# Grouped-query units moved beside the state-space scans, neighbourhood heads beside the Fourier mixer, weighted sums in float32

## The chip, the cores and the metric

The kernel runs on one core of a Trainium2 chip. Its engines each work through their own instructions in order: TensorE (PE, with its weight loads as PEld), VectorE (DVE), ScalarE (ACT), GpSimd (POOL), and SyncE (SP), which here issues DMAs. The metric is the device time of one execution in microseconds (us); lower is better.

## What is computed

Two layers of a hybrid block over 1,024 latent tokens and 256 context tokens (1,280 in all, ten tiles of 128), width 1,024. Each layer mixes tokens in four groups of 256 channels which share one input and one output projection, then runs an MLP:

```python
z = modulate(rms_norm(x, g_pre_mix), sh1, sc1) @ w_in         # latent; zc likewise for the context
oa = gqa_mixer(z, ...)      # A: 4 query heads on 2 key/value heads, softmax(q k) v, 64 channels a head
ob = s5_mixer(z, ...)       # B: 16 groups of 16 channels, 64 complex states, scan in both directions, GELU + GLU
on = na_mixer(z, ...)       # C: 4 heads, each query sees 8 x 16 grid neighbours (with a bias) and the context
od = fourier_mixer(z, ...)  # D: real 2-D DFT over positions and channels, then a linear map
y = jnp.concatenate([oa, ob, on, od], axis=-1) @ w_out
x = x + g1 * rms_norm(y, g_post_mix)
x = x + g2 * rms_norm(sq_relu_mlp(modulate(...), w_mlp1, w_mlp2), g_post_mlp)
```

Attention is a softmax of scores and then a weighted sum of the values `v`. The context's own outputs are needed in layer 0 only.

## The kernel before

Everything is computed to float32 accuracy. Most matmuls reach it by splitting each operand into a rounded high part and a low part, both of type fp32r, and adding three products (high x high, high x low, low x high), as in `mm3` (L157 to L162). ScalarE rounds (`copy`, L148), VectorE or GpSimd subtracts (`sub`, L151). S5's small matmuls are plain float32.

`run()` goes through a layer in stages: norm, input projection (with the preparation of S5's tables woven in), the middle stage, output projection (which starts with S5's gate matmuls, the GLU), MLP. The middle stage is what the change touches. It has two parts:

- `attention` works through *units*. A grouped unit G(j, b) is key/value head j with 512 queries of two query heads (b = 2: the 256 context queries, layer 0 only); an N(h) is one neighbourhood head. The order is `G(0,0), N(0), G(0,1), G(0,2), N(1), G(1,0), N(2), G(1,1), G(1,2), N(3)`. A unit's preparation (`gqa_prep`, `na_prep`: splitting, transposes, row maxima of the scores) is woven into the unit ahead of it. In a unit's main part (`gqa_main`, `na_main`), for each of ten key tiles: two fp32r score matmuls per 512 columns (L657, L795), the exponential on ScalarE (L658, L799) into `e`, and `weights`, which makes a rounded `eh` (ScalarE; every third key tile of a grouped unit VectorE, L607) and `el = e - eh` (shared by GpSimd and VectorE). One and two key tiles later `pv` issues three fp32r matmuls per block of 512 columns (L624, L625, L629) into the accumulator; `va` and `vl` are the values' high and low parts, and columns of ones in `va` make the softmax denominators. `finish` sends the denominators through memory and back with three DMAs (rt, den, rden), with a reciprocal between them, and multiplies.
- `s5_scan` then takes two of the 16 S5 groups at a time, beside the Fourier mixer `fnet` and the last unit's `finish`. `front` loads tables `v`, `cs`, `sn` by DMA on ScalarE's queue, multiplies (L1268), rotates, swaps the halves of the partitions, scans, rotates back; `rear` of a group comes two fronts later and makes its output with three matmuls (L1304, L1306).

`fnet` also fills the last unit's main part. The final order on each engine is that of a list scheduler with an internal timeline, given priorities in the code; score tiles have three PSUM banks (`ps_open("A", 3)`). After the stage the output projection loads its weights (`raw`, L170) on SP and splits them into `wh` and `wl`.

Of the kernel before, what the change touches and what calls it, by code (L numbers as in the profile page):

```python
# [26 lines left out]
NEG = -1.0e30  # L27
MAGIC = 12582912.0
# [3 lines left out]
class K:  # L32
# [72 lines left out]
    def ps_open(self, which, s1=0):  # L105
# [7 lines left out]
        if which == "A":  # L113
            self.psA, self.s1 = pool, s1
        else:
            self.psM = pool
# [336 lines left out]
    CM = [(part, off + m * 128, m) for part, off in (("naq", 768), ("nak", 1024), ("s5", 512), ("fn", 1536)) for m in range(2)]  # L453
# [32 lines left out]
    def qk_prep(self, p, ps, zg, t, cosr, sinr, gqk, h0):  # L486
# [12 lines left out]
        self.copy(zg[:, t, 384:512], ps[:, 384:512])  # L499
# [33 lines left out]
    def attn_set(self, p, nq, name, others=()):  # L533


        nc = self.nc
        s = {n: p.tile([128, w], F32R, name=name + n) for n, w in (("k1", TOK), ("k2", TOK), ("q1", nq), ("q2", nq))}
        for tag, w in others:
            p.tile([128, w], F32, tag=tag, bufs=1, name=tag)
        s["va"] = p.tile([128, NT, 128], F32R, name=name + "va")  # L540
        s["vl"] = p.tile([128, NT, 64], F32R, name=name + "vl")
        nc.gpsimd.memset(s["k2"][64:128, :].bitcast(F32), 0.0)
        nc.gpsimd.memset(s["k2"][64:65, :].bitcast(F32), 1.0)
        nc.gpsimd.memset(s["va"][:, :, 64:128].bitcast(F32), 1.0)
        return s

    def gqa_prep(self, st, u):

        nc, pb, s, zg = self.nc, st["pb"], st["g"], st["zg"]
        j, b, t0, n = u["j"], u["b"], u["t0"], u["n"]  # L550
        k1, k2, va, vl = s["k1"], s["k2"], s["va"], s["vl"]
        if b == 0:
# [8 lines left out]
            src = zg[:, :, 384 + 64 * j:448 + 64 * j]  # L561
            self.copy(va[:, :, 0:64], src)
            self.sub(vl, src, va[:, :, 0:64].bitcast(F32), nc.gpsimd)
# [8 lines left out]
        q1, q2 = st["c"] if b == 2 else (s["q1"], s["q2"])  # L572
# [27 lines left out]
        u["q"] = (q1, q2)  # L600
# [42 lines left out]
    def gqa_main(self, st, u, o):  # L643
        nc, pa, s = self.nc, st["pa"], st["g"]
        q1, q2 = u["q"]
        w = u["n"] * 128
# [1200 lines left out]
```

## Time and profile before

| | us |
|---|---|
| median of three runs | 3164.7 (3159.8 to 3165.99) |
| the profiled execution | 3155.56 |
| its span, first to last instruction | 3153.8 |
| TensorE busy | 2907.9 (92% of the span) |
| VectorE / ScalarE / GpSimd busy | 1824.3 / 1197.7 / 1194.1 |
| mean granted TensorE clock | 0.963 of full speed |

The median is over whole executions, the profile is one of them. Busy times are sums over the span and say nothing on their own of which engine others wait for; the middle stage takes 376.5 us of layer 0 and 343.5 us of layer 1 up to the output projection's first matmul.

### The profile page before, as it was taken

To read this page: it belongs to the slowest core of one execution; us is meant where nothing else is said; L and a number is where in the kernel's file an instruction comes from. 1 tells how busy PE (TensorE), PEld (TensorE's weight loads), DVE (VectorE), ACT (ScalarE), POOL (GpSimd) and SP (SyncE) were. 2 spreads that over 40 slices of the span, in tenths; PEclk is the share of its full clock that TensorE was granted. 3 is DMA by queue.
4 is the path that set the end of the run, shared out by engine and by line. 5 is a ranking of instruction groups with operands and counts; after the bars stand their busy time and mean duration, and the time that the engine had idled before them with its cause. 6 is when DMAs were issued, how large, how long until landed. Compare 5 with 4: busy or idle time off the path is not lost. (4 is left out here: it accounts for less than half of the span.)

```text
span 3153.8 us, 39690 instructions
## 1 busy us (share of the span) xinstructions
PE 2907.9 (92%) x15120; PEld 2450.9 (78%) x15120; DVE 1824.3 (58%) x2368; ACT 1197.7 (38%) x1932; POOL 1194.1 (38%) x951
## 2 busy tenths in 40 slices
PE   6999888789999999999999889878689999999998
PEld 3788666577888889888988788756577788888887
DVE  3465787586676544655554784689675334433334
ACT  3443666664322222332222244556663321212212
POOL 2474466445522122512212564466645211111113
PEclk8999999889999999999999999989889999999999
DMA  7534312562444432533333444411563211111113
GB/s 270 174 126 124 75 51 54 126 199 101 161 153 132 129 96 72 167 105 105 117 103 108 149 130 125 90 55 50 132 204 100 87 41 53 44 50 54 48 47 107
DMA packets 234723, 340.11 MB, mean 108 GB/s; under 512 B 50756, under 2 KB 170916, under 8 KB 234532
## 3 DMA queue, kind: packets, MB, share of 16 engines
q1 hardware_dynamic: 223268, 320.26, 33.0%
q10 hardware_dynamic: 11264, 17.31, 1.9%
q8 instruction: 119, 1.95, 0.3%
q14 instruction: 72, 0.59, 0.1%
HBM read 283.78 MB, written 53.62 MB: 107 GB/s over the span
## 5 line engine op out<-in xcount | busy, mean ns | idle before, releaser
L148 ACT ACTIVATE wh<-raw 128x1024 fp32r<-128x1024 f32 x234 | 242.6, 1056 | 787.2 <-PE ps L162 553.3
L160 PE MATMUL ps<-mh,wh 128*128 128x320 f32 (+1 forms) x1536 | 519.5, 338 | 9.4 <-DVE y L154 6.4
L162 PE MATMUL ps<-mh,wl 128*128 128x320 f32 (+1 forms) x1536 | 517.8, 337 | 0.9 <-DVE wl L151 0.9
L161 PE MATMUL ps<-ml,wh 128*128 128x320 f32 (+1 forms) x1536 | 518.1, 337 | 0.0
L154 DVE TENSOR_TENSOR y<-ps,y 128x1024 f32<-128x1024 f32 (+1 forms) x253 | 306.4, 1219 | 261.7 <-PE ps L162 261.5
L160 PE MATMUL ps<-wh,hidh 128*128 128x512 f32 x1152 | 452.0, 393 | 2.1 <-DVE y L154 2.1
L162 PE MATMUL ps<-wh,hidl 128*128 128x512 f32 x1152 | 448.2, 390 | 2.9 <-POOL hidl L151 2.9
L161 PE MATMUL ps<-wl,hidh 128*128 128x512 f32 x1152 | 449.7, 390 | 0.0
L151 POOL TENSOR_TENSOR hidl<-r,hidh 128x640 fp32r<-128x640 f32 (+1 forms) x128 | 189.3, 1479 | 679.0 <-DVE r L154 679.0
L151 DVE TENSOR_TENSOR wl<-raw,wh 128x1024 fp32r<-128x1024 f32 x188 | 289.2, 1551 | 167.4 <-ACT wh L148 162.9
L160 PEld LDWEIGHTS ps<-mh,wh 128*128 128x128 f32 x1536 | 290.2, 189 | 35.0 <-issue 7.3
L162 PEld LDWEIGHTS ps<-mh,wl 128*128 128x128 f32 x1536 | 289.9, 189 | 21.5 <-DVE wl L151 1.5
L161 PEld LDWEIGHTS ps<-ml,wh 128*128 128x128 f32 x1536 | 290.0, 189 | 20.7
L151 POOL TENSOR_TENSOR el<-e,eh 128x640 fp32r<-128x640 f32 (+7 forms) x164 | 250.5, 1540 | 131.7 <-ACT eh L148 44.7
L151 POOL TENSOR_TENSOR wl<-raw,wh 128x1024 fp32r<-128x1024 f32 x48 | 119.3, 2485 | 470.7 <-ACT wh L148 470.5
L160 PEld LDWEIGHTS ps<-wh,hidh 128*128 128x128 f32 x1152 | 216.8, 188 | 53.0 <-issue 5.8
L162 PEld LDWEIGHTS ps<-wh,hidl 128*128 128x128 f32 x1152 | 216.6, 188 | 49.1 <-POOL hidl L151 3.8
L161 PEld LDWEIGHTS ps<-wl,hidh 128*128 128x128 f32 x1152 | 216.8, 188 | 43.2
L154 DVE TENSOR_TENSOR r<-r 128x640 f32<-128x640 f32 (+1 forms) x128 | 96.7, 756 | 241.7 <-ACT hidh L1493 241.6
L1491 ACT ACTIVATE r<-ps 128x640 f32<-128x640 f32 (+1 forms) x128 | 82.3, 644 | 366.4 <-PE ps L162 360.2
L293 DVE SCALAR_TENSOR_TENSOR acc<-raw,cst,acc 128x1024 f32<-128x1024 f32 x70 | 98.0, 1424 | 139.2 <-DMA raw<-in_w_ada_dram 139.2
L151 DVE TENSOR_TENSOR el<-e,eh 128x384 fp32r<-128x384 f32 (+4 forms) x164 | 150.4, 926 | 42.7 <-ACT eh L148 25.9
(395 smaller groups left out, 5929.6 us busy)
## 6 DMA issues: line engine op xcount, KB each, us to landing
raw<-in_w_mlp_dram SPq DMA_DIRECT2D x192, 512.0 KB
raw<-in_w_ada_dram SPq DMA_DIRECT2D x96, 512.0 KB
raw<-in_w_in_dram SPq DMA_DIRECT2D x28, 512.0 KB
x<-x SPq DMA_DIRECT2D x26, 512.0 KB
x<-h SPq DMA_DIRECT2D x18, 512.0 KB
x<-in_x_dram SPq DMA_DIRECT2D x16, 512.0 KB
raw<-in_w_out_dram SPq DMA_DIRECT2D x16, 512.0 KB
bq<-in_na_bq_dram SPq DMA_DIRECT2D x8, 800.0 KB
```

The source lines that it names most:

```text
L148: self.nc.scalar.activation(out, in_, AF.Copy, scale=scale)
L151: (eng or self.nc.vector).tensor_tensor(out=out, in0=a, in1=b, op=OP.subtract)
L154: (eng or self.nc.vector).tensor_tensor(out=out, in0=a, in1=b, op=op)
L160: self.nc.tensor.matmul(ps, ah, bh, start=start and i == 0, stop=False)
L161: self.nc.tensor.matmul(ps, ah, bl, start=False, stop=False)
L162: self.nc.tensor.matmul(ps, al, bh, start=False, stop=stop and i == n - 1)
L293: nc.vector.scalar_tensor_tensor(acc[c], x, col, acc[c], op0=OP.mult, op1=OP.add)
L1491: nc.scalar.activation(r.rearrange("p (b n) -> p b n", b=nb), ps[:, :nb, :w], AF.Relu)
```

## The change

Five things change, all in the middle stage:

- Units run as all grouped ones first, then the four heads. Keys and queries have tiles of their own for each j and b, and heads have two sets in turn (`na_set`).
- The weighted sum is one float32 matmul per block on `e` itself. `weights`, `va` and `vl` go. The ones for the denominators are a 65th column beside each head's values, in `zg` and in `vf`.
- S5 works on one group at a time (16 steps), on single PSUM banks, and all its DMAs are issued by SP. A step of it follows every second step of a grouped unit; what is left is drained ahead of the unit that prepares the first head.
- `fnet` gets a step after every third step of a head. The last head's `finish` is drained at the end of `attention`.
- Scores have two PSUM banks instead of three; other tiles of one bank alternate between two pools. The input projection makes S5's columns ahead of the heads' (`CM`).

The diff, cut to its core:

```diff
-        pool, bufs = self.psM, 2
         if tag == "s1":
             pool, bufs = self.psA, self.s1
-        elif self.s1 == 3:
+        else:
+            where = self.p1[self.p1n % len(self.p1)]
             self.p1n += 1
-            if self.p1n % 3 == 0:
-                pool, bufs = self.psA, 1
+            pool, bufs = (self.psA if where == "A" else self.psM), 2
...
-    CM = [(part, off + m * 128, m) for part, off in (("naq", 768), ("nak", 1024), ("s5", 512), ("fn", 1536)) for m in range(2)]
+    CM = [(part, off + m * 128, m) for part, off in (("s5", 512), ("naq", 768), ("nak", 1024), ("fn", 1536)) for m in range(2)]
...
+    def na_set(self, pn, i):
+        nc = self.nc
+        s = dict(zip(("k1", "k2", "q1", "q2"), (*self.keys(pn, f"n{i}"), *self.queries(pn, f"n{i}", TOK))))
+        s["vf"], s["bt"] = pn.tile([128, NT, 65], F32, name=f"nvf{i}"), pn.tile([128, 23, 64], F32, name=f"nbt{i}")
...
-    def weights(self, pa, e, n, vec, lo):
-        eh = pa.tile([128, 1024], F32R, tag="eh", bufs=3, name="eh")[:, :n]
-        if vec:
-            self.nc.vector.tensor_copy(eh, e)
-        else:
-            self.copy(eh, e)
-        el = pa.tile([128, 1024], F32R, tag="el", bufs=3, name="el")[:, :n]
-        c = int(n * lo) // 64 * 64
-        self.sub(el[:, :n - c], e[:, :n - c], eh[:, :n - c].bitcast(F32), self.nc.gpsimd)
-        if c:
-            self.sub(el[:, n - c:], e[:, n - c:], eh[:, n - c:].bitcast(F32))
-        return eh, el
-    def pv(self, queue, s, kt, parts, start, stop):
-        mm = self.nc.tensor.matmul
-        def high():
-            for po, eh, el in parts:
-                mm(po, s["va"][:, kt, :], eh, start=start, stop=False)
-                mm(po[0:64], s["vl"][:, kt, :], eh, start=False, stop=False)
-        def low():
-            for po, eh, el in parts:
-                mm(po, s["va"][:, kt, :], el, start=False, stop=stop)
-        queue += [(2, high), (3, low)]
+        yield
+    def pv(self, queue, vf, kt, parts, start, stop):
+        def whole():
+            for po, e in parts:
+                self.nc.tensor.matmul(po[0:65], vf[:, kt, :], e, start=start, stop=stop)
+        queue.append((2, whole))
...
-            eh, el = self.weights(pa, e, 2 * w, kt % 3==1, 0.4)
-            parts = [(po[:, h * 512:h * 512 + w], eh[:, h * w:(h + 1) * w], el[:, h * w:(h + 1) * w]) for h in range(2)]
-            self.pv(queue, s, kt, parts, kt == kts[0], kt == NT - 1)
+            self.pv(queue, vf, kt, [(po[:, h * 512:h * 512 + w], e[:, h * w:(h + 1) * w]) for h in range(2)],
+                          kt == kts[0], kt == NT - 1)
...
-            eh, el = self.weights(pa, e, n, False, 0.3)
-            parts = [(po[:, x:y], eh[:, x - ra * 64:y - ra * 64], el[:, x - ra * 64:y - ra * 64]) for x, y in pieces]
-            self.pv(queue, s, kt, parts, i == 0, i == 9)
+            cols = [(po[:, x:y], slice(x - ra * 64, y - ra * 64)) for x, y in pieces]
+            self.pv(queue, s["vf"], kt, [(x, e[:, c]) for x, c in cols], i == 0, i == 9)
...
-        units = [G(0, 0), N(0), G(0, 1), G(0, 2), N(1), G(1, 0), N(2), G(1, 1), G(1, 2), N(3)]
+        units = [dict(kind="g", j=j, b=b, t0=4 * b, n=4 if b < 2 else 2) for j in range(2) for b in range(3)]
+        units += [dict(kind="n", h=h, nq=nq) for h in range(NA_HEADS)]
...
-    def attention(self, pa, fp, st, o, mid, late):
+    def attention(self, l, st, o, fnet):
...
+        sp = self.open(f"s5{l}")
+        side, every = self.s5_scan(sp, l), 2
+        self.ps_open("A", 2, "AM")
...
+            if sp is not None and any(units[k]["kind"] == "n" for k in ahead):
+                for _ in side:
+                    pass
+                sp.release()
+                sp = None
+                pn = st["pn"] = self.open(f"attN{l}")
+                st["n"] = [self.na_set(pn, 0)]
+            if i == ng:
+                for p in (pc, st["pb"], st["zp"]):
+                    p.release()
+                pa = self.open(f"attO{l}")
+                st["n"].append(self.na_set(pa, 1))
+                self.ps_open("A", 2, "A")
+                self.ps_open("M")
+                side, every = fnet, 3
...
-            if i + 1 < len(units):
-                self.weave(main, self.early(itertools.chain(*ahead), 600), 3)
-            else:
-                late = late()
-                for k, _ in enumerate(main):
-                    if k % self.late[1] < self.late[0]:
-                        next(late, None)
-        return st["fin"]
+            main = self.every(main, side, every)
+            self.weave(main, self.early(itertools.chain(*(self.attn_prep(st, k) for k in ahead)), 600), 3)
...
+        for _ in st["fin"]:
+            pass
...
+    def every(main, other, n):
+        for i, x in enumerate(main):
+            if i % n == n - 1:
+                next(other, None)
+            yield x
...
+        def front(g):
+            v, cs, sn = (p.tile([128, 2, w], F32, tag=n, bufs=2, name=n) for n, w in (("v", 128), ("cs", 160), ("sn", 160)))
             for t, n in ((v, "v"), (cs, "cs"), (sn, "sn")):
-                nc.scalar.dma_start(t, dr[n][:, g0:g0 + nb])
-            pv = self.ps2(tag="pS")
+                nc.sync.dma_start(t, dr[n][:, g])
...
-            nc.scalar.dma_start(dr["y"][g0:g0 + nb].rearrange("g p c -> p g c"), y)
+            nc.sync.dma_start(dr["y"][g], y)
...
-        for g0 in range(0, 16, nb):
-            st = (g0, front(g0))
-            if g0 < 2 * nb:
-                xs.append(outs(g0))
-            if g0 == nb:
-                t0 = p.tile([128, 16, 128], F32, tag="s5t0", bufs=1, name="s5t0")
+        for g in range(16):
+            st = (g, front(g))
+            if g < 2:
...
-            fnet, self.ftags = self.early(self.fnet(l, o), 100), ("pM",)
-            def late():
-                self.ps_open("M")
-                pb.release()
-                zp.release()
-                return fnet
-            self.ps_open("A", 3)
-            with self.pool(f"attA{l}") as pa:
-                fin = self.attention(pa, up, st, o, lambda: self.s5_load(s5u, l), late)
+            self.ftags = ("pM",)
+            st["zp"] = zp
+            self.attention(l, st, o, self.early(self.fnet(l, o), 100))
             self.ps_open("A")
-            self.npS, self.ftags = 1, ("pM", "pF")
-            with self.pool(f"s5{l}") as p:
-                for i, _ in enumerate(self.along(self.s5_scan(p, l, s5u), fin)):
-                    if i % self.mix == 0:
-                        next(fnet, None)
```

What moves on the engines. The first place is TensorE in layer 0's first grouped unit, before; `gq`/`gk` are queries and keys, numbers tell tiles apart, `nk`, `nq` belong to the next head's preparation.

```order
L629 MATMUL ps<-el,gva 128x512 x2
L657 MATMUL ps<-gq_2775,gk_2773 128x512
L657 MATMUL ps<-gq_2776,gk_2774 128x512
L624 MATMUL ps<-eh,gva 128x512
L625 MATMUL ps<-eh,gvl 64x512
L624 MATMUL ps<-eh,gva 128x512
L625 MATMUL ps<-eh,gvl 64x512
L657 MATMUL ps<-gq_2775,gk_2773 128x512
L657 MATMUL ps<-gq_2776,gk_2774 128x512
L748 MATMUL ps<-nk_3291,nq_3293 128x512
L629 MATMUL ps<-el,gva 128x512 x2
```

After, TensorE in layer 0's second grouped unit (`g0q`, `g0k` its queries and keys; `zg` holds values and ones; `s5u`, `v`, `z` are S5's input, table and scanned states, `z` of three tiles used in turn).

```order
L1268 MATMUL ps<-s5u,v 128x160 x2
L1299 MATMUL ps<-s5u,s5tm 128x160
L1301 MATMUL ps<-z_3352,x_3555 128x160 x2
L1268 MATMUL ps<-s5u,v 128x160 x2
L1299 MATMUL ps<-s5u,s5tm 128x160
L641 MATMUL ps<-g0q_2778,g0k_2774 128x512
L641 MATMUL ps<-g0q_2779,g0k_2775 128x512
L641 MATMUL ps<-g0q_2778,g0k_2774 128x512
L641 MATMUL ps<-g0q_2779,g0k_2775 128x512
L611 MATMUL ps<-e,zg 65x512 x2
L520 MATMUL ps<-identr,qhh 128x128 x4
L1301 MATMUL ps<-z_3350,x_3633 128x160 x2
```

Per block one float32 row on `e`,`zg` stands where rows with `eh` and `el` stood, and S5's rows stand among them: L1268 is the first matmul of a group, L1299 and L1301 are the last ones of an earlier group. The last row is of the group whose L1268 row is eight rows above the excerpt.

The second place is TensorE in S5 before, in layer 0:

```order
L1304 MATMUL ps<-s5u,s5tm 128x160
L1306 MATMUL ps<-z_6290,x_6332 128x160 x2
L1304 MATMUL ps<-s5u,s5tm 128x160
L1306 MATMUL ps<-z_6290,x_6332 128x160 x2
L1268 MATMUL ps<-s5u,v 128x160 x4
```

There, S5's rows stand by themselves, two groups after one another (four L1268 rows at a time) and beside the Fourier mixer's.

The third place is SP at the end of layer 0's middle stage, before; `raw` are weights of the output projection, `yt` S5's outputs, `gwr` the gate's weights:

```order
L1298 DMA x_6667<-s5x_147 128x512
L170 DMA raw<-in_w_out_dram 128x1024 x4
L1339 DMA yt_6739<-s5y_149 128x1280
L1339 DMA yt_6741<-s5y_149 128x1280
L1341 DMA gwr<-in_w_s_glu_dram 128x2x256
L195 DMA rg<-mod_2_82 128x1024
L195 DMA ra<-mod_4_84 128x1024
L195 DMA rb<-mod_3_83 128x1024
L170 DMA raw<-in_w_out_dram 128x1024 x4
```

After; `rt`, `den` and `rden` are the last head's denominators on their way to memory and back:

```order
L1334 DMA yt_6218<-s5y_149 128x1280
L1334 DMA yt_6220<-s5y_149 128x1280
L665 DMA rt<-rden 128x1x10
L1336 DMA gwr<-in_w_s_glu_dram 128x2x256
L194 DMA rg<-mod_2_82 128x1024
L194 DMA ra<-mod_4_84 128x1024
L194 DMA rb<-mod_3_83 128x1024
L672 DMA den_6160<-rt 128x10
L675 DMA rden<-den_6160 64x1280
L169 DMA raw<-in_w_out_dram 128x1024 x8
```

The first four loads of weights stood ahead of S5's outputs; all eight now stand behind the last denominators.

## Rows read from the trace of the kernel before

**Rows 1.** The page, busy time of the engines over the whole span.

```profile
PE 2907.9 (92%) x15120; PEld 2450.9 (78%) x15120; DVE 1824.3 (58%) x2368; ACT 1197.7 (38%) x1932; POOL 1194.1 (38%) x951
```

**Rows 2.** Stretches: length, PE PEld DVE ACT POOL busy (count), PEclk, DMA share, GB/s.

```profile
307.50:600.00 292.50, 241.64 (x1109) 180.17 (x1107) 226.44 (x373) 188.98 (x320) 171.46 (x122) 0.92 0.26 61
600.00:684.00 84.00, 60.39 (x334) 54.01 (x334) 60.17 (x104) 44.19 (x74) 45.93 (x44) 0.78 0.71 194
307.50:684.00 376.50, 302.03 (x1443) 234.18 (x1441) 286.61 (x476) 233.16 (x393) 217.39 (x165) 0.89 0.36 91
1986.00:2250.00 264.00, 219.52 (x966) 163.17 (x965) 214.16 (x342) 165.52 (x272) 158.79 (x106) 0.92 0.26 63
2250.00:2329.50 79.50, 53.72 (x318) 47.79 (x317) 57.35 (x99) 45.32 (x72) 50.38 (x48) 0.85 0.72 197
200.00:300.00 100.00, 90.74 (x607) 83.90 (x606) 62.55 (x132) 45.35 (x104) 59.01 (x63) 0.98 0.45 132
```

**Rows 3.** TensorE groups by form, 307.5 to 684 us: count, busy us, mean ns.

```profile
L624 PE MATMUL ps<-eh,gva 128*128 128x512 f32 x80 | 32.7, 409 | 1.2 <-ACT rden L148 1.2
```

**Rows 4.** TensorE timeline in a grouped unit: start, us, engine, line, tile.

```profile
340.84 0.40 PE L624 MATMUL ps<-eh,gva 128*128 128x512 f32 x1
341.07 0.39 PE L625 MATMUL ps<-eh,gvl 128*64 128x512 f32 x1
```

**Rows 5.** TensorE timeline in S5.

```profile
663.15 0.44 PE L1304 MATMUL ps<-s5u,s5tm 128*128 128x160 f32 x2
663.42 0.71 PE L1306 MATMUL ps<-z,x 128*128 128x160 f32 x4
663.96 0.43 PE L1304 MATMUL ps<-s5u,s5tm 128*128 128x160 f32 x2
```

**Rows 6.** Groups by form, 307.5 to 684 us, all engines.

```profile
L151 POOL TENSOR_TENSOR el<-e,eh 128x640 fp32r<-128x640 f32 x40 | 69.6, 1747 | 36.5 <-ACT eh L148 17.3 <-DVE eh L607 8.0 <-PE ps L657 4.7
...
L151 DVE TENSOR_TENSOR el<-e,eh 128x384 fp32r<-128x384 f32 x40 | 48.8, 1223 | 16.3 <-ACT eh L148 9.5 <-PE ps L657 3.3 <-ACT nmt L148 2.0
L658 ACT ACTIVATE e<-ps 128x512 f32<-128x512 f32 x80 | 45.3, 596 | 33.5 <-PE ps L657 23.8 <-DVE el L151 7.6 <-issue 0.8
L148 ACT ACTIVATE eh<-e 128x1024 fp32r<-128x1024 f32 x36 | 38.3, 1063 | 3.4 <-PE ps L625 3.0
```

**Rows 7.** Waits by line and releaser, 307.5 to 684 us: total us, times, longest.

```profile
POOL el L151 <- ACT eh L148: 26.3, 15, 5.7
...
PEld ps L629 <- POOL el L151: 14.8, 10, 4.3
...
PE ps L629 <- POOL el L151: 11.6, 6, 4.1
...
PE ps L1268 <- DMA v<-s5v: 8.2, 2, 7.5
```

**Rows 8.** S5 operations by form, same view and stretch as Rows 6.

```profile
L1283 DVE TENSOR_TENSOR_SCAN gg<-r,m 128x160 f32<-128x160 f32 x32 | 18.7, 639 | 0.1
...
L154 POOL TENSOR_TENSOR g<-gg,sn 128x640 f32<-128x640 f32 x8 | 14.4, 1796 | 18.1 <-issue 11.8 <-DMA v<-s5v 5.3 <-DVE gg L1283 0.9
...
L148 ACT ACTIVATE m<-m 64x640 f32<-64x640 f32 x16 | 11.8, 735 | 4.4 <-DVE m L154 2.0 <-DVE rt L688 1.9 <-DVE gl L151 0.3
```

**Rows 9.** SP timeline, issues of DMAs in layer 0.

```profile
362.72 0.52 SPq L682 DMA_DIRECT2D rt<-rden  x1
...
367.65 0.57 SPq L692 DMA_DIRECT2D rden<-den  x1
...
674.72 1.76 SPq L170 DMA_DIRECT2D raw<-in_w_out_dram  x4
...
689.81 2.44 SPq L170 DMA_DIRECT2D raw<-in_w_out_dram  x4
```

**Rows 10.** TensorE and GpSimd timeline at the end of the stage.

```profile
678.41 1.04 POOL L181 CAST wh<-raw 128x1024 fp32r<-128x1024 f32 x1 [0.26 <-DMA raw<-in_w_out_dram]
...
687.54 0.80 PE L161 MATMUL ps<-wl,oh 128*128 128x512 f32 x1 [2.00 <-DVE wl L151]
```

More of the change, by code (lines that the diff above doesn't have):

```diff
@@ L531, in put_o, with keys, queries @@
             pos, i = pos + m * step, i + m
-    def attn_set(self, p, nq, name, others=()):
+    def keys(self, p, name):
         nc = self.nc
[L537 to L544, printed above, removed]
+        k1, k2 = (p.tile([128, TOK], F32R, name=name + n) for n in ("k1", "k2"))
+        nc.gpsimd.memset(k2[64:128, :].bitcast(F32), 0.0)
+        nc.gpsimd.memset(k2[64:65, :].bitcast(F32), 1.0)
+        return k1, k2
+    def queries(self, p, name, n):
+        return [p.tile([128, n], F32R, name=name + x) for x in ("q1", "q2")]
+    def na_set(self, pn, i):
+        nc = self.nc
+        s = dict(zip(("k1", "k2", "q1", "q2"), (*self.keys(pn, f"n{i}"), *self.queries(pn, f"n{i}", TOK))))
+        s["vf"], s["bt"] = pn.tile([128, NT, 65], F32, name=f"nvf{i}"), pn.tile([128, 23, 64], F32, name=f"nbt{i}")
+        nc.gpsimd.memset(s["q2"][64:128, :].bitcast(F32), 0.0)
+        nc.gpsimd.memset(s["vf"][:, :, 64:65], 1.0)
         return s
     def gqa_prep(self, st, u):
-        nc, pb, s, zg = self.nc, st["pb"], st["g"], st["zg"]
+        nc, pb, zg = self.nc, st["pb"], st["zg"]
         j, b, t0, n = u["j"], u["b"], u["t0"], u["n"]
-        k1, k2, va, vl = s["k1"], s["k2"], s["va"], s["vl"]
+        k1, k2 = u["k"] = st["k"][j]
         if b == 0:
@@ L571, in gqa_prep @@
         yield
-        q1, q2 = st["c"] if b == 2 else (s["q1"], s["q2"])
+        q1, q2 = u["q"] = st["q"][b]
         self.transposes(q1, lambda i: qhh[:, i // n, i % n].rearrange("p a d -> p (a d)"), 2 * n)
@@ L655, in gqa_main @@
                 hs = slice(h * w, (h + 1) * w)
-                for kk, qq in ((s["k1"], q1), (s["k2"], q2)):
-                    nc.tensor.matmul(ps, kk[:, ks], qq[:, hs], start=kk is s["k1"], stop=kk is s["k2"])
+                for kk, qq in ((k1, q1), (k2, q2)):
+                    nc.tensor.matmul(ps, kk[:, ks], qq[:, hs], start=kk is k1, stop=kk is k2)
                 nc.scalar.activation(e[:, hs], ps, AF.Exp)
@@ L730, in na_prep @@
         yield
[L731 to L734 removed]
+        mx = pn.tile([128, 8, 3], F32, tag="mx", bufs=1, name="mx")
         nc.gpsimd.memset(mx, NEG)
@@ L832, in attn_start @@
         nq = NLAT if l == self.depth - 1 else TOK
-        st = dict(l=l, pb=pb, zg=zg, g=self.attn_set(pb, 1024, "g"))
+        st = dict(l=l, pb=pb, zg=zg, k=[self.keys(pb, "g0")], q=[self.queries(pb, "g0", 1024)])
         st["ql"] = pb.tile([128, 2, 4, 128], F32R, name="ql")
         self.nc.gpsimd.memset(st["ql"][:, :, :, 64:128].bitcast(F32), 0.0)
-        G = lambda j, b: dict(kind="g", j=j, b=b, t0=4 * b, n=4 if b < 2 else 2)
-        N = lambda h: dict(kind="n", h=h, nq=nq)
-        units = [G(0, 0), N(0), G(0, 1), G(0, 2), N(1), G(1, 0), N(2), G(1, 1), G(1, 2), N(3)]
+        units = [dict(kind="g", j=j, b=b, t0=4 * b, n=4 if b < 2 else 2) for j in range(2) for b in range(3)]
+        units += [dict(kind="n", h=h, nq=nq) for h in range(NA_HEADS)]
         st["units"] = [u for u in units if u.get("b") != 2 or nq > NLAT]
@@ L844, in attn_prep @@
         return self.gqa_prep(st, u) if u["kind"] == "g" else self.na_prep(st, u)
-    def attention(self, pa, fp, st, o, mid, late):
+    def attention(self, l, st, o, fnet):
         units = st["units"]
-        nq = units[1]["nq"]
-        st["pa"], st["fp"], st["n"] = pa, fp, self.attn_set(pa, TOK, "n", (("bq", 25 * 64), ("cq1", 512), ("cq2", 512), ("bt", 23 * 64)))
-        self.nc.gpsimd.memset(st["n"]["q2"][64:128, :].bitcast(F32), 0.0)
-        st["c"] = [pa.tile([128, 512], F32R, tag=f"c{n}", bufs=1, name=f"c{n}") for n in ("q1", "q2")] if nq > NLAT else None
+        ng = sum(u["kind"] == "g" for u in units)
+        ctx = any(u.get("b") == 2 for u in units)
+        up = self.open(f"up{l}")
+        for n, w in (("oraw", TOK), ("rden", TOK), ("oraw2", 256), ("rden2", 512)):
+            up.tile([128, w], F32, tag=n, bufs=1, name=n)
+        pg = self.open(f"attG{l}")
+        st["fp"], st["pg"] = up, pg
+        pc = self.open(f"attC{l}", "right")
+        st["k"].append(self.keys(pc, "g1"))
+        st["q"].append(self.queries(pc, "g1", 1024))
+        if ctx:
+            st["q"].append(self.queries(pc, "gc", 512))
+        sp = self.open(f"s5{l}")
+        side, every = self.s5_scan(sp, l), 2
+        self.ps_open("A", 2, "AM")
         for i, u in enumerate(units):
-            if i == len(units) // 2:
-                mid()
             ahead = [] if u.get("b") == 2 else [i + 1]
@@ L1263, in front @@
+        def front(g):
+            v, cs, sn = (p.tile([128, 2, w], F32, tag=n, bufs=2, name=n) for n, w in (("v", 128), ("cs", 160), ("sn", 160)))
             for t, n in ((v, "v"), (cs, "cs"), (sn, "sn")):
[L1264 to L1265 removed]
+                nc.sync.dma_start(t, dr[n][:, g])
+            pv = self.ps1()[:, :320].rearrange("p (d c) -> p d c", d=2)
             for d in range(2):
[L1267 to L1269 removed]
@@ L1270, in front @@
-            pv = pv.rearrange("p (d c) -> p d c", d=2)[:, :, :nb * 160].rearrange("p d (g c) -> p g d c", g=nb)
-            m1, m2, m3 = (p.tile([128, nb, 2, 160], F32, tag=n + par, bufs=1, name=n) for n in ("m1", "m2", "m3"))
+                nc.tensor.matmul(pv[:, d], v[:, d, :], u[:, g, 32 * d:32 * d + 160], start=True, stop=True)
+            m1, m2, m3 = (p.tile([128, 2, 160], F32, tag=n, bufs=2, name=n) for n in ("m1", "m2", "m3"))
+            self.tt(m2, pv, sn, OP.mult)
             self.tt(m1, pv, cs, OP.mult)
-            self.tt(m2, pv, sn, OP.mult)
```

141 lines of the change are left out of this document (60 added, 81 removed).

## The prediction

> **What bounds the kernel now.** I read the page first. TensorE is busy 92% of the span and no other engine over 58% [rows 1], but that mixes stages, so I cut the span where the change acts: per layer, from the first score matmul to the moment at which the output projection's matmuls run without gaps, 307.5 to 687.5 us in layer 0 and 1986.2 to 2332.7 in layer 1 (380 and 346.5 us; by [rows 10] the first of these matmuls starts at 687.54, and the bounds in layer 1 are found in the same way). The table by stretches [rows 2] shows two things there that the input projection (200 to 300 us) does not have: a granted clock of 0.92 and 0.78 (0.92 and 0.85 in layer 1) against 0.98, and an S5 part in which TensorE is busy for 60 of 84 us.
>
> Busy time is modelled and stretches at the lower clock, so I also counted what TensorE would need at its full pace. A reduced-precision (fp32r) matmul of 512 columns starts 0.23 us after the one ahead of it [rows 4]; by the median over all neighbours it is 0.227, and 0.120 for 256 columns, 0.11 for 128. A float32 matmul leaves two records; three rows of S5 have two records of 160 columns in 0.27 us and four in 0.54 [rows 5], 0.135 each, which is two clocks a column at 2.4 GHz. With these paces the 1443 matmuls of the first window [rows 2], and the few up to 687.5, need 246 us, and layer 1's need 227. So the stage uses 65% of its time for matmuls in both layers; counted likewise, the input projection uses 85% (84.6 of 100 us). The rest is waiting: the list of waits has TensorE and its weight loads on the weights' low parts (14.8 + 11.6 us), GpSimd for the rounded weights (26.3), and S5's first matmul for a table (8.2) [rows 7]. No engine is full; they wait for one another in turn.
>
> **The change, part by part.**
>
> *Weighted sums.* Three fp32r matmuls per block of 512 columns, 3 x 0.227 = 0.681 us, become one float32 matmul of two records. By [rows 5] a 512-column record is 512 x 2 / 2.4 GHz = 0.427 us, the pair 0.854. Per layer the blocks are 80 of 512 in the grouped units [rows 3], 50 in the heads (four heads of 6,400 columns), and in layer 0 eight of 256 in each kind for the context: 138 and 130 in units of 512. TensorE pays 268 x 0.173 = 46 us: 246 becomes 270, 227 becomes 249.5. The price is bounded below by the pace of two fp32r matmuls (0.454, 61 us less than now) and above by twice the pair (1.7); 0.854 is taken, being the row's own form at another width.
>
> The Trainium skill (page "FP8 and Floating Point Precision", section "TensorE Precision Notes") has true FP32 as four passes through the array. Four passes at the fp32r pace of 0.227 would make 0.908 in place of 0.854, an estimate, and the sum 14 us dearer. No row here has a float32 matmul of 512 columns; S5's rows show two records for one matmul, not four.
>
> *What goes from the other engines.* In layer 0: 64 us of rounding copies on ScalarE (38.3 of them in one row), 90 on VectorE (48.8 in one row, the rest in narrower ones and in casts), 137 on GpSimd (69.6 in one) [rows 6]. Their load in the stage falls from 233, 287 and 217 us [rows 2] to about 170, 198 and 80. TensorE at 270 is then clearly the longest. The chain from an exponential to its weighted sum also loses a copy (1.06 us) and a subtraction (1.75 us on GpSimd).
>
> *S5 among the grouped units.* The same matmuls in pieces of one group. Its VectorE and ScalarE operations are half as wide and twice as many: a swap of 0.735 us at 640 columns becomes two of between 0.37 and 0.735; I take 0.43, so 32 x 0.125 = 4 us more per layer on ScalarE, hidden since it is not full; uncovered it would be those 4 us. VectorE's and GpSimd's halves I take as halves. One group's chain (two products, swap, difference, two scans of 0.64, product, swap, product, three sums) is about 8 us by halves of [rows 8]. In the new order a group's last matmuls stand two or three fronts behind its first, but sometimes only 5 to 8 us of matmuls, as the excerpt of the change shows: TensorE then waits in order, and score and weighted-sum matmuls behind it wait too. I allow 1 us for each of the 16 groups; it lies in the share used below.
>
> *Loads.* 64 issues of S5 tables and outputs go from ScalarE to SP, and 80 are added by halving the pieces. SP gets some 72 per layer at about 0.45 us, 32 us spread over 190. Their cover is that fronts run two groups ahead, about 12 us each. Behind a unit's denominators an S5 load can wait the 4.9 us from the one issue to the other [rows 9]; that is less than the cover, so nothing is charged. The transfers themselves move from a stretch with a DMA share of 0.71 into ones with 0.26 [rows 2]. Without cover it would be 6 units x 5 us = 30 us per layer.
>
> *Two score banks in place of three.* An exponential takes 0.60 us, a pair of score matmuls 0.45. The 1.7 us of weighted sums lies between, so it is hidden; without it, 0.15 us per bank.
>
> *Charged at nothing.* The order of the input projection's columns, tiles of their own for keys and queries, the memsets of ones, two sets for the heads: the same work or less, on engines with room, under a TensorE that is busy. Uncovered, the memsets are a few us per layer.
>
> *The end.* Before, the projection's first weights were issued at 674.72, under the last S5 groups, and the second four at 689.81 [rows 9]; the full pace came at 687.54. After, all eight stand on SP behind the last head's denominators. After the last weighted sum come copies out of the accumulator, the 4.9 us between issues, then landing (3.7 us from the issue at 674.72 to the first cast of these weights on GpSimd [rows 9, 10]), rounding and difference: about 13 us by an estimate, of which S5's gate matmuls fill 4. I charge 9 us per layer. It is between 3 (what before loses now) and 30 (denominators, S5 outputs and loads one after the other, at the lower clock after the gap).
>
> **Sum.** In layer 0 the grouped units with S5 hold 161 us of matmuls (scores 38, weighted sums 72, preparations 26, S5 22, one head's preparation 3), the heads with the Fourier mixer 109. Grouped units: many independent matmuls, other engines at 60 to 65% of it; I choose the input projection's kind of share, 86%: 187 us. Heads: bias additions, maxima and a chain of single-row copies remain, so I choose 79%, between that and the 70% which before's attention uses (203.6 us of matmuls at full pace in the 292.5 of [rows 2]): 138 us. 187 + 138 + 9 = 334, 46 less than 380. Layer 1: 151 / 0.86 + 98.5 / 0.79 + 9 = 310, 36 less. Together 82 us off the profiled execution's 3155.6, so 3073. The median of the three runs is 9 us above that execution, so 3080 to 3082 there; I say 3080. Other stages run the same work.
>
> **Rivals.**
>
> *Denser than I think.* If the waits of [rows 7] vanish and TensorE runs at 93% throughout, the stage takes 270 / 0.93 + 9 = 299 and 277 us: 150 less, 3014. For it: with three helpers far from full, hardly anything else can bind. Against: in-order waits on S5 chains, and heads that keep their chains.
>
> *The gain is lost at the ends.* The last head runs without a partner, since the Fourier mixer's pieces are used up by the third, and the loads come late: 30 us per layer in place of 9 leaves 40 us, 3124. For it: the low clock of 0.78 in the stretch 600 to 684, whose end is exposed likewise [rows 2].
>
> *Slower: S5 holds TensorE.* Each of the 32 groups' last matmuls waits in the in-order stream until its chain is done. The gain of 82 us is gone at 2.6 us more per group than I allow; at 4 us it is 128 - 82 = 46 us slower, 3210. For it: the chain of 8 us against as little as 5 us of matmuls between; against: in most places two units' matmuls lie between.
>
> *Nothing gained.* The stage's share rises only as much as float32 costs: 380 and 346.5 stay, 3165. The share would be 71%, which attention alone has now.
>
> **Chances.** My forecast 0.55, with a range of its own from 3045 to 3120 (the shares 5 points higher or lower move it by 35 to 40 us); denser 0.16; lost at the ends 0.16; slower 0.08; nothing gained 0.05. 0.2% is 6 us, about what a measurement of this kernel tells from no change. Faster holds the first three, less a little for ends dearer still: 0.85; same 0.05; slower 0.10. The range leaves out the densest cases and the slower one: 3028 to 3150.
>
> **What would show it.** Right: score and weighted-sum matmuls back to back, the float32 pair of 512 columns at 0.85 us; the stage at 334 and 310 us; granted clock above 0.95 in the grouped units; GpSimd down by about 250 us over the span; 9 us between the last weighted sum and the projection's pace. Wrong: S5's last matmuls (line 1301) with waits for GpSimd's sums of several us, a float32 pair at over 0.95 us, heads at under 70%, or a gap of over 20 us ahead of the projection.

## The result and the profile after

The changed kernel takes 3114.5 us (median of 4 runs, 3110.3 to 3118.3) against 3162.3 before; the ratio is 0.985 (0.983 to 0.988), 48 us less where 85 were forecast. The profiled execution has a span of 3108.5 us against 3153.8.

The page after, engines over the span, answers to [rows 1]:

```profile
PE 2899.1 (93%) x14816; PEld 2361.5 (76%) x14816; DVE 1640.4 (53%) x2240; ACT 1094.7 (35%) x1856; POOL 938.2 (30%) x847
```

GpSimd lost 256 us of work, VectorE 184, ScalarE 103. TensorE's own line hardly moved, so the question is where it waits. The table by stretches after (length, busy time and count of PE, PEld, DVE, ACT, POOL, granted clock, DMA share, GB/s), cut where the work changes, answers to [rows 2]:

```profile
299.60:319.20 19.60, 9.04 (x36) 5.83 (x35) 8.38 (x15) 2.30 (x4) 2.32 (x2) 0.67 1.10 141
319.20:496.00 176.80, 161.49 (x668) 98.60 (x667) 104.61 (x206) 107.47 (x207) 45.61 (x79) 0.98 0.39 93
496.00:643.00 147.00, 124.97 (x582) 81.14 (x582) 85.24 (x186) 67.22 (x135) 37.92 (x32) 0.90 0.37 104
643.00:670.40 27.40, 12.31 (x43) 9.88 (x43) 19.79 (x48) 20.51 (x50) 10.95 (x11) 0.50 0.43 156
1955.70:1976.00 20.30, 11.34 (x48) 7.17 (x47) 7.70 (x19) 7.29 (x12) 2.32 (x2) 0.90 1.09 129
1976.00:2145.00 169.00, 150.23 (x593) 90.66 (x591) 90.06 (x176) 94.50 (x180) 45.58 (x78) 0.95 0.38 94
2145.00:2273.00 128.00, 111.39 (x501) 70.41 (x499) 82.14 (x185) 59.28 (x114) 31.48 (x30) 0.92 0.44 122
2273.00:2297.50 24.50, 10.28 (x37) 8.57 (x38) 17.49 (x42) 17.47 (x43) 9.85 (x10) 0.56 0.35 121
```

The four stretches of a layer are its start, the grouped units with S5, the heads with the Fourier mixer, and the end up to the projection. The middle two are what was hoped for: a clock of 0.98 and 0.95 in the grouped units, and matmuls at full pace (counted as in the prediction) fill 154 of 176.8 us, 87%, and 141.5 of 169, 84%. The first and last stretch of each layer have a low clock or a DMA share of 1.1, and hold 5.0 and 8.3 us of matmuls in 20, and 5.0 and 4.5 in 27 and 24.

The **start**. TensorE's timeline and SP's (start, us, engine, line) and the DMA view of 299.6 to 319.2 us:

```profile
317.50 1.43 PE L1268 MATMUL ps<-s5u,v 128*128 128x160 f32 x4 [7.53 <-DMA v<-s5v]
```
```profile
301.18 0.42 SPq L1238 DMA_DIRECT2D s5u<-u  x1
...
311.79 0.34 SPq L1265 DMA_DIRECT2D v<-s5v  x1
```
```profile
DMA packets 5078, 2.76 MB, mean 141 GB/s; under 512 B 2274, under 2 KB 4949, under 8 KB 5077
```

S5's first matmul stands ahead of most of the first unit's scores, and its table `v` stands on SP behind 14 loads of `s5u`. These are 5,078 packets, almost all under 2 KB; the DMA engines are full while only 141 GB/s move. TensorE waits 7.5 us for the table. The granted clock is 1.00 until 304 us and 0.50 (1.2 GHz) from 307 to 324; it had fallen ahead of the long wait, and from 301 to 307 us only short waits for VectorE's row maxima stand between the matmuls.

Most of this loss is not new. The kernel before, in the same length from its first score on (stretch, then a wait of TensorE):

```profile
307.50:327.10 19.60, 11.92 (x43) 8.30 (x41) 14.32 (x25) 7.93 (x11) 5.15 (x3) 0.74 1.11 179
```
```profile
PE ps L739 <- DVE nk L151: 3.7, 1, 3.7
```

There too the DMA engines were full (the same loads of `s5u` were issued from 300.9 to 323.7 us, between others for the first head), and TensorE was without matmuls for some 13 us of 19.6 by the same count, and 11 of 20.3 in layer 1. It waited for the first head's keys and the first exponentials; now it waits for S5's table.

The **end**. SP, GpSimd, VectorE and TensorE at the end of layer 0:

```profile
643.91 0.51 SPq L665 DMA_DIRECT2D rt<-rden  x1
...
652.37 0.46 SPq L675 DMA_DIRECT2D rden<-den  x1
652.92 22.37 SPq L169 DMA_DIRECT2D raw<-in_w_out_dram  x8
```
```profile
664.13 0.96 POOL L1357 TENSOR_SCALAR tf<-w 128x256 f32<-128x256 f32 x1 [2.02 <-DVE w L1352]
665.04 1.03 POOL L180 CAST wh<-raw 128x1024 fp32r<-128x1024 f32 x1
```
```profile
670.12 4.82 DVE L150 TENSOR_TENSOR wl<-raw,wh 128x1024 fp32r<-128x1024 f32 x4
```
```profile
641.11 1.97 PE L611 MATMUL ps<-ec,nvf 128*65 128x256 f32 x4 [2.42 <-DVE rden L785]
648.63 0.79 PE L159 MATMUL ps<-th,gwh 128*128 128x256 f32 x2 [5.56 <-ACT th L147]
...
670.43 1.05 PE L159 MATMUL ps<-wh,oh 128*128 128x512 f32 x2
```

The denominators take 8.5 us from the first issue to the last where [rows 9] had 4.9, and the weights' loads stand behind them. Two stretches (as in the table) show when these land:

```profile
653.00:661.00 8.00, 3.94 (x13) 3.06 (x13) 5.52 (x12) 5.74 (x16) 4.42 (x5) 0.50 0.84 303
661.00:671.00 10.00, 5.46 (x19) 4.34 (x19) 8.01 (x20) 6.64 (x14) 4.62 (x5) 0.50 0.00 0
```

The first four blocks, issued from 652.92 to 654.46, are there by 661 us, 8 us after the first issue where 3.7 were reckoned with for one; after that nothing moves until the fifth is issued at 671.36. So for the last 9 us the weights are there, and their rounding is late: on GpSimd (665.04) it stands behind the gate's `tf`, on ScalarE (667.63) and VectorE (670.12) behind other operations of the gate. Between the last weighted sum and the projection lie 27 us, in which only the gate's matmuls run.

The float32 sum itself, two records of one matmul, then the next work:

```profile
330.56 1.02 PE L611 MATMUL ps<-e,zg 128*65 128x512 f32 x2
331.42 0.70 PE L1268 MATMUL ps<-s5u,v 128*128 128x160 f32 x4
```

0.86 us, against 0.854 in the sum. The Trainium skill's four passes ("FP8 and Floating Point Precision", "TensorE Precision Notes") agree if a pass costs its columns alone: 4 x 512 / 2.4 GHz is 0.853, an estimate; the dearer one of 0.908 had taken four times the fp32r matmul's pace of 0.227, which is 0.014 above 512 / 2.4 GHz.

### The profile page after: what moved, and what is told of

Read it like the earlier page. It is cut to its first block, busy times and chain, and to the rows that moved or that the text cites. A ratio compares the mean times of both kernels' runs of the same rounds, so it can differ in the third digit from the quotient of the medians.

```text
span 3108.5 us, 38660 instructions
## 1 busy us (share of the span) xinstructions
PE 2899.1 (93%) x14816; PEld 2361.5 (76%) x14816; DVE 1640.4 (53%) x2240; ACT 1094.7 (35%) x1856; POOL 938.2 (30%) x847
## 4 chain that ended last, share of the span: by engine, by line
PE 56%; DVE 6%; DMA 5%; issue 3%; POOL 3%; ACT 2%; SPq 0%; DVEq 0%; POOLq 0%; ACTq 0%
PE ps L159 17%; PE ps L161 17%; PE ps L160 17%; PE ps L611 2%; DMA raw<-in_w_ada_dram 1%; DVE wl L150 1%; DVE y L153 1%; PE ps L772 1%; POOL rs L215 1%; PE ps L641 1%; DMA raw<-in_w_mlp_dram 0%; DVE acc L292 0%; DMA s5u<-u 0%; DVE y L1390 0%; DMA kd<-zn 0%
## 5 line engine op out<-in xcount | busy, mean ns | idle before, releaser
L611 PE MATMUL ps<-e,zg 128*65 128x512 f32 (+1 forms) x336 | 170.7, 598 | 3.8 <-DVE rden L653 2.8
L159 PE MATMUL ps<-hh,wh 128*128 128x320 f32 (+1 forms) x480 | 151.5, 316 | 2.7 <-ACT vst L147 2.7
```

Of the source, the lines that this page charges most:

```text
L159: self.nc.tensor.matmul(ps, ah, bh, start=start and i == 0, stop=False)
L611: self.nc.tensor.matmul(po[0:65], vf[:, kt, :], e, start=start, stop=stop)
```

## Experiments

Each ratio is to the kernel before, timed beside it (medians of 3158 to 3161 us, 3162 beside the changed kernel); the changed kernel's own ratio is 0.985 (0.983 to 0.988). The expectations number some kernels: the first has S5 later, the second the weights early, the seventh S5 later with the copy on GpSimd, the eighth the gate in the last head, the ninth the denominators on GpSimd, the tenth and twelfth the further edits of the end.

**The float32 sums alone**, in the old order of units (kernel before, `weights`, `va` and `vl` gone, `e` with four buffers):

```diff
-                mm(po, s["va"][:, kt, :], eh, start=start, stop=False)
-                mm(po[0:64], s["vl"][:, kt, :], eh, start=False, stop=False)
...
-        queue += [(2, high), (3, low)]
+                mm(po[0:65], s["va"][:, kt, :], e, start=start, stop=stop)
+        queue.append((2, high))
```

> The kernel before with the float32 weighted sums alone: order of units, S5 and Fourier mixer as before. Theory 1 (the helpers' roundings and subtractions were the wait, so float32 makes the gain and the new order little more): attention falls from 292 us by some 25 per layer, 3162 becomes about 3112. Rival (waits were those of the units' chains, which the order alone mends): TensorE's 23 us per layer of dearer sums are not paid back, 3160 to 3200.

3131.2 us, ratio 0.991 (0.990 to 0.992): 28 us less, between the two. The row of the stage to 671 us shows the helpers relieved just as in the changed kernel, with GpSimd at 80 us where [rows 2] have 217:

```profile
304.70:671.00 366.30, 307.71 (x1287) 199.59 (x1286) 206.15 (x382) 181.15 (x322) 80.44 (x72) 0.89 0.38 95
```

The clock is 0.89 as before, but TensorE is denser: the matmuls with float32 sums (270 us in the prediction's count) fill 74% of these 366 us, where 246 filled 65% of 380 before and 274 fill 74% of 371 in the changed kernel. So the sums are worth some 28 us, and the new order the 17 that remain; the new order without the sums was not run. These 17 do not lie in the middle stage. From the first grouped score to the projection's first matmul, the kernel before takes 377 and 343 us in its two layers, this one 363 and 336, the changed kernel 371 and 341. What the changed kernel has ahead of this one comes behind that: the projection, first matmul to last, takes 122 and 96 us in place of 136 and 105. Another 5 us lie ahead of layer 0's stage.

**S5 later.** `every(main, side, every, 8 if i == 0 else 0)`: no S5 step in the first eight steps of the first unit.

> The changed kernel with one edit: S5's first step comes only after the eighth step of the first grouped unit, so that its first matmul no longer stands ahead of that unit's second score matmul. Theory 1 (15 us per layer are lost at the stage's start, because TensorE waits in order for S5's loads): the 7.5 us wait at 310 to 317 us and its slow clock go, some 12 us per layer less, 3114 becomes about 3090. Rival (S5's chain is what the grouped units need time for, so starting it later only moves the wait to the drain ahead of the first head): 3108 to 3120.

3126.9 us, 0.990 (0.988 to 0.992): slower than the changed kernel by 12, so both were wrong in size. The first float32 sum came 15 us after the input projection's last matmul in place of 25, but then ScalarE's timeline shows:

```profile
333.87 3.86 ACT L147 ACTIVATE s5tm<-s5t 128x2048 f32<-128x2048 f32 x1 [13.60 <-DMA s5t<-s5e]
337.54 1.10 ACT L642 ACTIVATE e<-ps 128x512 f32<-128x512 f32 x2
```

The same loads, now waited for on ScalarE, with the exponentials behind. Next the same with that copy on GpSimd (`nc.gpsimd.tensor_copy(tm..., t0...)`):

> S5's first step after the eighth step of the first grouped unit, as in the first experiment, and the copy that rearranges S5's table s5tm on GpSimd instead of ScalarE. Theory 1 (the loads of S5's inputs and of s5tm, some 6,000 small packets, take till 30 us into the stage whatever stands behind them; in the first experiment the wait moved from TensorE's first S5 matmul to ScalarE's copy of s5tm, with 13 us before the exponentials behind it): with the copy on an idle engine the wait of 13 us goes and with it 10 to 13 us per layer of the first experiment's 3127, to 3100 to 3108. Rival (starting S5 late costs the same at its end, where the heads' preparation waits for its memory): 3115 to 3127.

3108.7 us, 0.983 (0.981 to 0.985). The wait is gone and 18 us of the first attempt are back, but against the changed kernel 6 us remain, which the two intervals do not tell from nothing. In layer 0 the first sum comes 9 us earlier and the heads' first scores 1.5 us earlier only (201 us after the input projection's last matmul, 202 in the changed kernel); in layer 1 the heads come 6 us earlier (198, 204), while the first sum is where it was (11 us).

**Is it S5's end that sets the heads' start?** The seventh kernel with an S5 step after every step (`side, every = self.s5_scan(sp, l), 1`):

> The seventh kernel (S5 late by eight steps, s5tm on GpSimd) with an S5 step after every step of a grouped unit instead of every second. In all kernels of the new order the first head's scores start 31 to 38 us after S5's last matmul, since the head's preparation takes S5's memory. Theory 1 (S5's end plus that preparation sets where the grouped part ends): S5 ends 20 to 40 us earlier and the heads start 5 to 10 us earlier per layer, 3108 becomes 3090 to 3100. Rival (TensorE is already at 87% there and the coincidence comes from the order in which the units are written): 3104 to 3112; and if S5's chain of 8 us per group holds TensorE when groups follow closely, above 3115.

3119.0 us, 0.987 (0.985 to 0.989). S5's last matmul came 142 us after the input projection's last one in place of 167, the heads 208 in place of 201. In layer 1 S5 ended 29 us earlier and the heads came 4 us earlier (194, 198). The theory falls in layer 0 and holds in small part at best in layer 1: heads don't start when S5 lets them, and S5 more closely spaced costs rather than gains.

**The Fourier mixer spread over four heads** (`side, every = fnet, 4`):

> The changed kernel with one edit: a Fourier step after every fourth step of a head in place of every third, so that the last head has a partner too. Theory 1 (heads at 74% of full pace because the fourth runs alone): 3 to 5 us per layer less, about 3106. Rival (a head's own chains set its time; the Fourier mixer's late end then stands in the exposed end): 3112 to 3125.

3114.6 us, 0.986 (0.984 to 0.987): no difference. But the edit did not do what it was meant to: the mixer's last matmul comes at 624.8 us and the last head's first score at 626.7 (2244.2 and 2258.6 in layer 1), so the last head still runs alone, and whether that costs anything stays untested. The changed kernel's own trace says where the heads lose most. The first one:

```profile
501.70:546.30 44.60, 31.81 (x138) 20.90 (x136) 23.32 (x53) 16.16 (x36) 8.80 (x15) 0.78 0.49 139
```

Its matmuls at full pace would take some 26 of these 44.6 us, 19 less; in layer 1 the first head loses some 12 of 41 us. The last heads lose 8 and 2.

**Denominators on GpSimd's queue** (`nc.sync.dma_start` to `nc.gpsimd.dma_start` three times in `finish`). The reason lay in SP's timeline of the changed kernel and in its waits (us in total, times, longest) from 496 to 643 us: the mixer's first input stands behind a denominator, and TensorE waits.

```profile
521.15 0.51 SPq L675 DMA_DIRECT2D rden<-den  x1
521.76 7.05 SPq L911 DMA_DIRECT2D u<-uf  x3
```
```profile
PE ps L159 <- ACT uh L147: 7.7, 1, 7.7
```

> The changed kernel with the three DMAs of every unit's denominators issued by GpSimd instead of SP. Theory 1 (loads of the next work stand on SP behind issues that wait for denominators: the Fourier mixer's first input in layer 0, which costs 7.7 us, and the projection's weights, some 9 us at each layer's end): 20 to 25 us less, about 3090. Rival (loads come too late for other reasons, the transfers themselves and the engines' order): 3108 to 3120. If issuing on GpSimd is dear, its products for S5 come late and the time is above 3120.

3108.8 us, 0.984 (0.983 to 0.986), 6 us less at most. The wait for the mixer's input is 4.5 us in place of 7.7; the end stays at 26 us, though the first weights are issued 5 us ahead of the last weighted sum instead of 10 us behind it. GpSimd's rounding of the first block stands behind the gate's `tf` again (666.71). The queue did not set the end.

**The end**, in four kernels. First, the first four blocks of weights are loaded during the last head, into a pool opened where the mixer's memory was:

```diff
+            if i == len(units) - 1:
+                for _ in fnet:
+                    pass
+                wr, order = self.open(f"wr{l}", "right"), (0, 1, 4, 5)
+                raws = [wr.tile([128, 1024], F32, name=f"wr{k}") for k in order]
+                for k, r in zip(order, raws):
+                    self.nc.sync.dma_start(r, self.a["w_out"][l, k * 128:(k + 1) * 128, :])
```

> The changed kernel with one edit: the first four blocks of the output projection's weights are loaded during the last head, into memory that the Fourier mixer has left. Theory 1 (the stage's end, 27 and 24 us from the last weighted sum to the projection's pace, waits for weights that stand on SP behind the last denominators): the end falls to 15 to 18 us, some 18 us off 3114, about 3096. Rival (the end is set by the last head's denominators and by the gate's chain on ScalarE and VectorE): no more than 3 us per layer, 3108 to 3118.

3127.5 us, 0.990 (0.988 to 0.992), slower by 13. The loads of these four were issued 34 us ahead of the last sum, so they were not what the end waited for. ScalarE rounded the blocks, the later four too, among the gate's operations and ahead of the mixer output's first tile (`oh`), and TensorE waited for that:

```profile
611.19 2.79 SPq L866 DMA_DIRECT2D wr<-in_w_out_dram  x4
```
```profile
665.44 2.94 ACT L147 ACTIVATE wh<-raw 128x1024 fp32r<-128x1024 f32 x3
668.28 2.37 ACT L147 ACTIVATE oh<-o 128x256 fp32r<-128x256 f32 x6
```
```profile
668.83 0.76 PE L159 MATMUL ps<-wh,oh 128*128 128x512 f32 x1 [6.35 <-ACT oh L147]
```

The gap fell by 4 us in layer 0, and the projection, with the gate's later matmuls now in it, took 8 us more. So the gate too goes into the last head (`side, every = self.glu(gp, l, o), 4`, its pool on the right):

> The early loads of the second experiment, and S5's gate (gelu, gate matmuls) woven into the last head, a step after every fourth step, ahead of the output projection. Theory 1 (what stands between the last weighted sum and the projection's pace are the gate's operations on ScalarE and VectorE, ahead of the splitting of weights in these engines' order): the end of 24 to 27 us falls to 14 to 18, and the projection has no gate matmuls in it; 15 us per layer less, about 3085 to 3095. Rival (the last head's denominators and product set the end): 3105 to 3120. Second rival (ScalarE changes its function table between exponential and tanh in the last head): over 3125.

3138.8 us, 0.993 (0.992 to 0.995). The time is above 3125, but the second rival's mechanism did not happen: no table load of ScalarE lies in the heads of either layer. In layer 0 the last head grew by some 11 us, in layer 1 the heads by 17, and the gaps were still 21 and 22: ScalarE and TensorE at the end of layer 0,

```profile
672.44 1.06 ACT L147 ACTIVATE wh<-raw 128x1024 fp32r<-128x1024 f32 x1 [12.07 <-DMA raw<-in_w_out_dram]
```
```profile
677.78 0.76 PE L159 MATMUL ps<-wh,oh 128*128 128x512 f32 x1 [21.07 <-ACT oh L147]
```

The rounding of a later block, whose load is late, stands on ScalarE ahead of the first tile's. The next kernel splits the later blocks after that tile and has the denominators on GpSimd:

> Three edits for the stage's end at once: weights loaded early and S5's gate in the last head (as in the eighth kernel), denominators' DMAs on GpSimd (as in the ninth), and the later four blocks of weights split only after the first tile of the mixer's output. In the eighth kernel ScalarE waited 12 us for the loads of the later weights with that tile's rounding behind it, and those loads stood on SP behind the denominators. Theory 1 (the end is a row of in-order waits, and each one taken away alone uncovers the next): with all three gone the gap after the last weighted sum falls from 21 to 27 us to some 14, the last denominators' way; against the changed kernel's 3114 about 3090 to 3100. Rival (work moved into the last head lengthens it by as much as the end loses, as the eighth kernel's 11 us show): 3108 to 3125.

3111.7 us, 0.985 (0.983 to 0.988). GpSimd and SP show what was left, and that it was this edit's own: the later blocks had been put into the memory of the last head's sums, and waited for its product.

```profile
661.90 3.02 POOL L153 TENSOR_TENSOR o<-oraw,rden 64x640 f32<-64x640 f32 x2 [3.67 <-DMA rden<-den]
```
```profile
664.95 2.07 SPq L169 DMA_DIRECT2D raw<-in_w_out_dram  x4
```

With a pool `uz` of their own for those sums, no rounding on GpSimd, and the last head's channels last (`order = (0, 1, 4, 6, 7, 2, 3, 5)`):

> The tenth kernel with what its trace shows still in the way at the end taken away: the last head's sums and denominators lie in memory of their own, so that the later four weight loads need not wait for the last product on GpSimd (in the tenth they were issued 13 us after the last weighted sum); no rounding of weights on GpSimd behind that product; and the projection takes the last head's channels last. Theory 1 (the end is a row of in-order waits that can all be taken off TensorE's path): TensorE starts the projection some 5 us after the last weighted sum in place of 19 to 28, 12 us per layer less than the tenth's 3112, about 3085 to 3092. Rival (the last head's product is needed early on all the same, or the splitting of eight weights on ScalarE and VectorE, 8 to 10 us, sets the pace): 3100 to 3112.

3101.5 us, 0.982 (0.980 to 0.985), 10 us below the changed kernel by the ratios, at the edge of what these runs tell. TensorE's timeline:

```profile
653.50 1.08 PE L611 MATMUL ps<-ec,nvf 128*65 128x256 f32 x4 [0.93 <-DVE rden L785]
660.48 0.79 PE L159 MATMUL ps<-wh,oh 128*128 128x512 f32 x1 [5.89 <-ACT oh L147]
...
677.08 0.79 PE L159 MATMUL ps<-wh,oh 128*128 128x512 f32 x1 [5.79 <-ACT wh L147]
```

The gap is 6 us where it was 28 (from the last weighted sum's start), 22 less in layer 0. Of that the heads with the gate take 7 and the projection 10: 3 us of gain there. Layer 1 has 19 us less in the gap; heads and what is ahead of them take 4 of it, the projection 8.

> The twelfth kernel and the seventh together (S5 starts eight steps late, its table s5tm is rearranged on GpSimd). If the two ends of the stage are separate losses, the sum of both differences: some 6 us less than the twelfth. If a gain at the start is given back by the order that follows, as in the first and the eleventh kernel, the same as the twelfth within 5 us.

3098.0 us, 0.981 (0.978 to 0.983): the fastest here, 15 us below the changed kernel by the ratios. The gap stays at 7 us in both layers. The step from the twelfth is 3 us, too little to tell the two expectations apart.

## Why the prediction was right in direction and too large

- *TensorE becomes the bound in the grouped units*: right. The share forecast was 86%, measured 87 and 84%; the pair at 0.86 us was priced at 0.854; layer 0's matmuls come to 274 us with the gate's 4, 270 forecast without. What the helpers lost in work was right too. But the float32 sums alone, with the same relief, make TensorE as dense as the changed kernel's (74% of the stage) and gain 28 us: before, chains of waits bound the stage, and these go only in part with the load.
- *S5's matmuls hold TensorE* (the slower rival): did not happen. The waits of line 1301 for GpSimd add up to 1.2 us in layer 0's grouped part and 3.5 in layer 1's.
- *Loads, "nothing is charged"*, and the share of 86% from the first score on: **here the start was missed.** The prediction gave the grouped units from their first matmul on the share of a stretch in steady work, and took a mean DMA share of 0.26 [rows 2] for room, while in the first 20 us of the kernel before that share is 1.11. The start holds 14.6 us without matmuls in layer 0 and 12 in layer 1, where 86% leaves 3 each. Some 13 and 11 of them were there before, so the loads that moved under the grouped units cost 1 or 2 us there; the term that was left out is a start that the stage had all along. The mixer's first input, which cost 7.7 us in layer 0, stood right behind a denominator on SP in the kernel before too (580.93 and 581.56 us); TensorE waited 0.6 us for it there, and 6.7 with the float32 sums alone in the old order. So this wait came with the sums, not with the new order.
- *The end, 9 us*: **too small by 18 and 16 us**; the rival of the exposed end, at 30, was near, and a gap of over 20 us was one of the prediction's own signs of being wrong. **This step failed too**, in what it left out. It had been worked out as a chain of denominators, one load and its rounding (13 us), with the gate as 4 us of matmuls that fill it. In layer 0 the denominators took 3.6 us more, the first four loads together some 4 more than one, and from 661 to 670.4 us the rounding stood behind the gate's operations on ScalarE, VectorE and GpSimd, which had been put at nothing. Some of it comes back: the projection is 11 and 9 us shorter. In layer 0, 42 of the gate's 60 matmuls have moved into the gap, some 5 us at full pace, and TensorE's waits within the projection, 8 us before, are gone. This return was not in the sum.
- *Heads at 79%*: 74.5 and 77%, 9 and 3 us more. The first head of each layer loses most, in layer 0 with the 7.7 us for the mixer's input; that the last one runs alone was not tested.
- The sum: over grouped units with the start, heads and end, layer 0 took 9 + 9 + 18 us more than forecast, layer 1 13 + 3 + 16, together 68 of the 82. The stage itself gained 9 and 5 us. The projection's 20 and some 10 us in other stretches (4 of them ahead of the input projection of layer 0, whose work did not change) make the 45 of the profile. That the total came to more than half of the forecast is in part luck: the stage gave 14 of the 82 us, and the projection's 20 were not forecast.

Still open: why starting S5 later gives back in the grouped units most of what it saves at the start. The waits after it are spread over many lines of 1 to 6 us, and the kernel in which S5 ends early has heads 7 us later in layer 0 and 4 us earlier in layer 1. Only the order of engines, which comes out anew with every edit, was seen to differ.

## What to carry to other kernels

When the busy part of a stage is to get denser, look at its two ends first, in the trace of the kernel before already: a share taken from a stretch in steady work does not hold them, and a mean over the stage hides them. Here the starts and ends of two layers hold 69 us without matmuls (14.6, 12.0, 22.4 and 20.0). Most of the starts' 27 were in the kernel before; the ends' 42 are what the middle of the old stage had hidden (the last chain of denominators, the gate, the next stage's weights). The wait at the end had no single cause: it took early loads, the gate moved, the splits reordered, a separate piece of memory and another order of channels together, while early loads alone, the gate with them, and the denominators' queue alone gave nothing that can be told, or lost. After each step, the trace names the next instruction that stands in order ahead of the wanted one. That a load is issued late does not show that it is waited for: in layer 0 the first weights had landed 9 us ahead of the projection.

## What the runs showed of the hardware

The loads at the start kept the DMA engines full (a share of 1.10 and 1.09) at 141 and 129 GB/s; in layer 0 these were 5,078 packets, 4,949 of them under 2 KB. At the end, with blocks of 512 KB, 303 GB/s moved at a share of 0.84. A float32 matmul of 512 columns takes 0.86 us in a row of others, as two records. Giving another engine the issue of some DMAs moved little (6 us at most), as the Trainium skill has it ("Trainium Kernel Development and Optimization", "Key Constraints": queues of several engines share the same 16 DMA engines, and only issue time is saved); denominators issued by GpSimd took 0.5 to 0.6 us each of its time.
